# Seven block products for eight in both SwiGLU up projections, and a residual that lives in DRAM

## The chip, the cores and the metric

The kernel runs on one core of a Trainium2 chip. TensorE (PE) multiplies matrices into PSUM; VectorE (DVE), ScalarE (ACT) and GpSimd (POOL) compute element by element; SyncE (SP) issues DMAs. Each engine works through its own instructions in order, and semaphores tie the engines together. The metric is the time of one execution on the device in microseconds (us); the median of the runs is compared.

## The reference

A trunk of two layers on 1024 frames of 1024 channels: a mixer and a SwiGLU network each, both added to a residual `h`. The mixers (a convolution with pooling in layer 0, the HGRN2 recurrence in layer 1) compute what they did before. The hidden width D_FF is 2816. All is float32.

```
def rmsnorm(x, g):
    xf = x.astype(jnp.float32)
    y = xf * lax.rsqrt(jnp.mean(xf * xf, axis=-1, keepdims=True) + EPS)
    return (y * g.astype(jnp.float32)).astype(x.dtype)
...
def swiglu_ffn(h, w1, w3, w2):
    return (jax.nn.silu(h @ w1) * (h @ w3)) @ w2
...
    h = x
    for layer in range(DEPTH):
        hn = rmsnorm(h, norm_mix_g[layer])
...
        h = h + mix
        h = h + swiglu_ffn(rmsnorm(h, norm_ffn_g[layer]), ffn_w1[layer], ffn_w3[layer], ffn_w2[layer])
    return rmsnorm(h, final_g)
```

## The kernel before

Everything is kept with the channels on the 128 partitions and the frames along the free axis, in two halves `hf` of H = 512 frames. The residual is 16 SBUF tiles `hT[k][hf]` (8 channel groups k by 2 halves). Each large product has both operands split in a high and a low part (`split`, `load`: ACT casts the high part, DVE subtracts to get the low part) and is made in three passes, high by high, high by low, low by high (`gemm_steps`, L156 to L158). A product of one output tile over 8 channel groups is thus 24 matmuls of 128x512.

`Norm.gather` takes a finished residual tile, squares it on ACT (L218), adds the squares up on GpSimd (L220) and splits the tile times the norm's gain (L172, L173). The division by the RMS is applied later, to what the product gives: `rows` makes the broadcast tile `bcs`, by a chain of small DVE instructions, two products on TensorE and an ACT copy.

`ffn` walks over 22 hidden tiles j of 128 in blocks of 2, 4, 4, 4, 4, 4 (BLOCKS). For a hidden tile it loads the columns of w1 and w3 (512 KB each) and makes four products, p1 and p3 for both halves: 96 matmuls. DVE multiplies each by the RMS row (L586, L588), ACT applies the SiLU (L587), DVE multiplies the two (L589) and the result is split (L169, L170). At a block's end `down` multiplies the block's hidden tiles by w2: 16 output tiles, in a block of four of 12 matmuls each, and DVE adds each from PSUM to the residual (`add_residual`, L243). In the last block `norm_next.gather` follows each tile.

Products go on TensorE in the order of the program text (each behind the last one by `issue_after`); the other engines' instructions are put in order by a scheduler from the same text, and the tile pools set when buffers come free. Raw weights have two buffers (NRAW), their high and low parts three each (NSPLIT). Products take PSUM from four "g" banks (`gbank`), small things from four "m" banks. The page and its answers leave out the numbers in names, so `f0p` is any p1 or p3 of layer 0, `f0o` any down product there, and `wr`, `wh`, `wl` are a weight block raw, high and low.

## Time and profile before

| | before |
|---|---|
| median of 3 runs | 2366.84 us (2366.27 to 2366.86) |
| span of the profiled execution | 2363.6 us |
| PE busy | 2326.9 us, 98% |
| DVE busy | 1345.2 us, 57% |
| ACT busy | 600.5 us, 25% |
| POOL busy | 91.2 us, 4% |

The span is the time from the first to the last instruction of one profiled execution; the median of the timed runs is 3.2 us longer. Busy time is the time in which an engine executes an instruction. Slices of the span show PE at nine tenths or more from the second to the next-to-last fortieth. The rows below come from views of that execution: the page; the busy time by stretch (windows); the waits of an engine with what ended them; groups of instructions by line; and the timeline, where each row has a start, a duration, and in brackets the idle time before it and the instruction that ended it.

### The profile page before, as it was taken

What the parts mean: (1) busy time and instruction counts of PE and PEld (TensorE: products, weight loads), DVE (VectorE), ACT (ScalarE), POOL (GpSimd) and SP (SyncE); (2) the same over time, 40 slices, a digit from 0 to 9 for tenths busy, and PEclk for the clock granted to TensorE, in tenths of its full rate; (3) what the DMA queues carried; (4) which work ended last, traced back from release to release, by engine and by line L of the source; (5) the groups of instructions that cost most, each with busy time, mean ns of one, the idle gap of its engine ahead of it and who ended that gap; (6) DMA issues with size and microseconds to landing.
All of it is one profiled execution on the core that took longest, in us unless ns stands there. A gap on an engine that the chain in (4) does not pass through costs nothing.

```text
span 2363.6 us, 27955 instructions
## 1 busy us (share of the span) xinstructions
PE 2326.9 (98%) x11342; PEld 1959.9 (83%) x11342; DVE 1345.2 (57%) x2539; ACT 600.5 (25%) x962; POOL 91.2 (4%) x67
## 2 busy tenths in 40 slices
PE   8999999999999999999999999999999999999998
PEld 6887878888888888888898889887888888888888
DVE  7999953333333333567877778798433333333337
ACT  5223521112121211333232222215121211112126
POOL 1030200000000000110000000003000000000000
PEclk9999999999999999999999999999999999999999
DMA  4101211111111111121111111112111111111114
GB/s 155 55 24 50 72 54 45 54 45 46 44 53 54 45 54 45 63 72 46 36 46 36 54 45 45 37 36 63 40 50 54 45 54 45 54 41 51 53 45 143
DMA packets 181792, 126.89 MB, mean 54 GB/s; under 512 B 4692, under 2 KB 174880, under 8 KB 181664
## 3 DMA queue, kind: packets, MB, share of 16 engines
q1 hardware_dynamic: 181296, 124.94, 17.4%
q8 instruction: 89, 1.46, 0.2%
q14 instruction: 39, 0.32, 0.0%
q10 hardware_dynamic: 368, 0.17, 0.0%
HBM read 119.85 MB, written 4.19 MB: 52 GB/s over the span
## 4 chain that ended last, share of the span: by engine, by line
PE 89%; DVE 7%; issue 2%; ACT 1%; DMA 1%; SPq 0%; DVEq 0%; ACTq 0%
PE f1p L158 7%; PE f1p L156 7%; PE f1p L157 7%; PE f0p L156 7%; PE f0p L157 7%; PE f0p L158 7%; PE f1o L156 3%; PE f1o L158 3%; PE f1o L157 3%; PE f0o L157 3%; PE f0o L156 3%; PE f0o L158 3%; PE pl L750 3%; DVE y L375 2%; PE pq L156 1%
## 5 line engine op out<-in xcount | busy, mean ns | idle before, releaser
L138 ACT CAST wh<-wr 128x1024 fp32r<-128x1024 f32 x218 | 229.4, 1052 | 801.8 <-PE f1o L157 173.4
L139 DVE TENSOR_TENSOR wl<-wr,wh 128x1024 fp32r<-128x1024 f32 x216 | 267.9, 1240 | 33.9 <-ACT wh L138 33.3
L158 PE MATMUL f1p<-hn_nf_0h,wl 128*128 128x512 f32 x352 | 137.9, 392 | 3.3 <-DVE wl L139 3.3
L156 PE MATMUL f0p<-hn_nf_1h,wh 128*128 128x512 f32 x352 | 138.0, 392 | 0.0
L156 PE MATMUL f1p<-hn_nf_0h,wh 128*128 128x512 f32 x352 | 137.8, 392 | 0.1
L157 PE MATMUL f0p<-hn_nf_1l,wh 128*128 128x512 f32 x352 | 137.9, 392 | 0.0
L158 PE MATMUL f0p<-hn_nf_1h,wl 128*128 128x512 f32 x352 | 137.8, 392 | 0.0
L157 PE MATMUL f1p<-hn_nf_0l,wh 128*128 128x512 f32 x352 | 137.5, 390 | 0.0
L156 PE MATMUL f0p<-hn_nf_0h,wh 128*128 128x512 f32 x352 | 137.1, 389 | 0.0
L156 PE MATMUL f1p<-hn_nf_1h,wh 128*128 128x512 f32 x352 | 137.1, 389 | 0.0
L157 PE MATMUL f0p<-hn_nf_0l,wh 128*128 128x512 f32 x352 | 137.0, 389 | 0.0
L157 PE MATMUL f1p<-hn_nf_1l,wh 128*128 128x512 f32 x352 | 137.0, 389 | 0.0
L158 PE MATMUL f1p<-hn_nf_1h,wl 128*128 128x512 f32 x352 | 137.0, 389 | 0.0
L158 PE MATMUL f0p<-hn_nf_0h,wl 128*128 128x512 f32 x352 | 136.9, 389 | 0.0
L243 DVE TENSOR_TENSOR h<-h,f1o 128x512 f32<-128x512 f32 (+1 forms) x104 | 66.8, 645 | 115.3 <-PE f1o L158 114.9
L375 DVE SCALAR_TENSOR_TENSOR y<-a,dww,y 128x512 f32<-128x512 f32 (+1 forms) x150 | 130.8, 918 | 0.4
L243 DVE TENSOR_TENSOR h<-h,f0o 128x512 f32<-128x512 f32 x96 | 65.6, 684 | 110.6 <-PE f0o L158 110.5
L588 DVE TENSOR_TENSOR f1u<-f1p,bcs_nf 128x512 f32<-128x512 f32 x44 | 30.4, 691 | 170.0 <-PE f1p L158 170.0
L588 DVE TENSOR_TENSOR f0u<-f0p,bcs_nf 128x512 f32<-128x512 f32 x44 | 30.4, 691 | 170.0 <-PE f0p L158 170.0
L768 DVE COPY_PREDICATED S<-masks,pl 128x128 f32<-128x128 uint8 x288 | 94.1, 341 | 12.0 <-PE pl L750 10.4
L586 DVE TENSOR_TENSOR f1s<-f1p,bcs_nf 128x512 f32<-128x512 f32 x44 | 30.4, 692 | 106.0 <-PE f1p L158 104.5
L586 DVE TENSOR_TENSOR f0s<-f0p,bcs_nf 128x512 f32<-128x512 f32 x44 | 30.4, 691 | 105.7 <-PE f0p L158 104.1
(432 smaller groups left out, 5596.7 us busy)
## 6 DMA issues: line engine op xcount, KB each, us to landing
wr<-in_ffn_w SPq DMA_DIRECT2D x144, 512.0 KB, 3.7
wr<-in_hg_w_in SPq DMA_DIRECT2D x40, 512.0 KB, 4.0
wr<-in_cp_w_in SPq DMA_DIRECT2D x12, 512.0 KB, 3.9
wr<-in_cp_w_out SPq DMA_DIRECT2D x12, 512.0 KB, 3.4
wr<-in_hg_w_out SPq DMA_DIRECT2D x10, 512.0 KB, 3.7
x<-in_x SPq DMA_DIRECT2D x16, 256.0 KB, 5.6
out<-ob SPq DMA_DIRECT2D x8, 512.0 KB, 3.3
band<-in_c_band SPq DMA_DIRECT2D x1, 512.0 KB, 4.8
```

The source lines that it names most:

```text
L138: nc.scalar.copy(wh, raw)
L139: (leng or nc.vector).tensor_tensor(wl, raw, f32(wh), ALU.subtract)
L156: nc.tensor.matmul(ps, lh, xh, start=k == 0, stop=False)
L157: nc.tensor.matmul(ps, lh, xl, start=False, stop=False)
L158: mm = nc.tensor.matmul(ps, ll, xh, start=False, stop=k == len(xs) - 1)
L243: nc.vector.tensor_tensor(h, h, ps, ALU.add)
L375: nc.vector.scalar_tensor_tensor(acc, tap(at, j, t0, n), dww[:, j, c:c + 1], acc, ALU.mult, ALU.add)
L586: nc.vector.tensor_tensor(s, p1, rs[hf], ALU.mult)
L588: nc.vector.tensor_tensor(u, p3, rs[hf], ALU.mult)
L750: nc.tensor.matmul(pl[:, c], K[:, ch[cc]], M[:, :, cc * 64:(cc + 1) * 64], start=True, stop=True)
L768: nc.vector.copy_predicated(sv, mk.unsqueeze(1).to_broadcast([P, 2, 64 // w, w]), pl[:, :, j, :].rearrange("p c (b n) -> p c b n", n=w))
```

## The change

**Seven products.** With w1 and w3 side by side and both operands cut in two, the four outputs of a hidden tile, w1 and w3 by the two halves of frames, form a product of 2x2 blocks: even and odd channel groups are the inner blocks, the two weights the outer ones on one side, the halves of frames on the other. The class `Up` forms it in the Winograd form of Strassen's method: seven products of 12 matmuls, 84 for a hidden tile, on sums of blocks. The operand sums (`b11, b21, b22, t1..t4`) are made once for a layer in `PairNorm.gather`, per pair of residual tiles, when the second half's tiles are finished. The weight sums (s23: two blocks, one by GpSimd; s4; a2 in place) are made for each hidden tile by `sums`, and the output sums by `p1`, `p2` and `rest`: seven DVE additions from PSUM and an ACT copy in place of none. In the first block both hidden tiles' p1 and p2 go first, then the rest. Odd products take "g" banks, even ones "m" banks.

**The residual in DRAM.** The 16 SBUF tiles are gone; NACT, the ring of 512-frame tiles, grows from 48 to 72. The residual is `hd`, 8 DRAM tiles of 512 KB. A down product of all blocks but the last is copied from PSUM by ACT to a tile of the ring `su` (three of 128x1024, shared with the hidden tile's s and u), and GpSimd issues a DMA of 512 KB that adds it to `hd`. The mixer's first out-projection ("op", 16 tiles) and the HGRN2 out-projections (40 tiles) do the same in 256 KB through the ring `tmp` of three. Where a norm follows, the residual tile is fetched two ahead on SP's queue, added to by DVE, gathered and written back on ACT's queue. The HGRN2 out-projection of heads 4 to 7 for the second half of frames is made in one at the end.

```diff
-    NACT, NRAW, NSPLIT = 48, 2, 3
+    NACT, NRAW, NSPLIT = 72, 2, 3
...
+    def sooner(n=400):
+
+        return tc.high_priority(offset=n)
...
-    hT = [[hpool.tile([P, H], F32, tag=f"h{k}_{hf}", name=f"h{k}_{hf}") for hf in range(NH)] for k in range(KT)]
+    hd = [dram.tile([P, T], F32, name=f"hd{k}") for k in range(KT)]
...
+    class PairNorm(Norm):
...
+            if hf == 0:
+                z = ("b11", "b21")[k % 2]
+                ops[z][i] = split(h, f"{nm}{z}_{i}", scale=self.gain(k))
+            if hf == 0 or k % 2 == 0:
+                return
+            ge, go = self.gain(k - 1), self.gain(k)
+            (h11, h21), (h12, h22) = (x[k - 1:k + 1] for x in self.h)
+            t1 = temp(f"{nm}t1r_{i}")
+            nc.vector.tensor_tensor(t1, h12, h11, ALU.subtract)
+            nc.scalar.activation(t1, t1, AF.Copy, scale=ge)
+            ops["t1"][i] = split(t1, f"{nm}t1_{i}")
+            t2 = temp(f"{nm}t2r_{i}")
+            nc.vector.scalar_tensor_tensor(t2, h22, go, t1, ALU.mult, ALU.subtract)
+            ops["t2"][i] = split(t2, f"{nm}t2_{i}")
+            t4 = temp(f"{nm}t4r_{i}")
+            nc.vector.scalar_tensor_tensor(t4, h21, go, t2, ALU.mult, ALU.subtract)
+            ops["t4"][i] = split(t4, f"{nm}t4_{i}")
+            t3 = temp(f"{nm}t3r_{i}")
+            nc.scalar.activation(t3, h12, AF.Copy, scale=ge)
+            nc.vector.scalar_tensor_tensor(t3, h22, go, t3, ALU.mult, ALU.subtract)
+            ops["t3"][i] = split(t3, f"{nm}t3_{i}")
+            ops["b22"][i] = split(h22, f"{nm}b22_{i}", scale=go)
...
+    def accumulate(k, hf, ps, name):
+
+        o = temp(f"ev_{name}{k}_{hf}")
+        nc.scalar.copy(o, ps)
+        nc.gpsimd.dma_start(out=hd[k][:, half(hf)], in_=o, accum_op=ALU.add)
+
+    def fetch(k, hf, name):
+        h = staged(f"h_{name}{k}_{hf}")
+        nc.sync.dma_start(out=h, in_=hd[k][:, half(hf)])
+        return h
...
+    def add_residual(h, ps, t0=0, n=H):
+        nc.vector.tensor_tensor(h[:, t0:t0 + n], h[:, t0:t0 + n], ps, ALU.add)
+
+    def put_back(k, hf, h, eng=nc.scalar):
+        eng.dma_start(out=hd[k][:, half(hf)], in_=h)
...
-                            add_residual(2 * m2 + mo, hf, po)
-            # layer norm over the channels, then swish
+                            accumulate(2 * m2 + mo, hf, po, "op")
...
+        def wide(name):
+            return pool.tile([P, T], F32, tag="su", name=name, bufs=3)
+
+        class Up:
...
+            def sums(self):
+                self.fetch("w3", w3, self.tile("wraw", "w3", NRAW))
+                x = pool.tile([P, 1024], F32, tag="s23", name=f"{self.nm}s23", bufs=1)
+                xv = x.rearrange("p (two i b) -> p two i b", two=2, b=P)
+                a1, a2 = (self.raw[z].rearrange("p (i two b) -> p two i b", two=2, b=P) for z in ("w1", "w3"))
+                nc.gpsimd.tensor_tensor(xv[:, 1], a1[:, 0], a2[:, 0], ALU.subtract)
+                nc.vector.tensor_tensor(a2[:, 0], a2[:, 0], a2[:, 1], ALU.add)
+                nc.vector.tensor_tensor(xv[:, 0], a2[:, 0], a1[:, 0], ALU.subtract)
+                c = self.cast(self.run(x), "s23")
+                self.w[6], self.w[7] = (tuple(t[:, i:i + 4] for t in c) for i in (0, 4))
+                self.parts(self.cast(self.run(self.raw["w3"]), "a2"), 5, 4)
+                nc.vector.tensor_tensor(a1[:, 1], a1[:, 1], xv[:, 0], ALU.subtract)
+                self.w[3] = self.cast(a1[:, 1], "s4", 512)
+
+            def product(self, i):
+                xs = norm.ops[("b11", "b21", "b22", "t4", "t1", "t2", "t3")[i - 1]]
+                wh, wl = self.w[i]
+                ps = (gbank if i % 2 else mbank)(f"{self.nm}p{i}")
+                for k, (xh, xl) in enumerate(xs):
...
+            def p1(self):
+                self.r1 = (staged if self.first else temp)(f"{self.nm}p1")
+                nc.scalar.copy(self.r1, self.product(1))
...
+            def rest(self, scales=lambda: None):
...
+                nc.vector.tensor_tensor(u2, self.r1, self.product(6), ALU.add)
+                nc.vector.tensor_tensor(u3, u2, self.product(7), ALU.add)
+                nc.vector.tensor_tensor(self.u[:, l], u3, self.product(4), ALU.add)
+                if not self.first:
+                    self.gate(0, self.c11)
+                p5 = self.product(5)
+                nc.vector.tensor_tensor(u2, u2, p5, ALU.add)
+                nc.vector.tensor_tensor(self.u[:, r], u3, p5, ALU.add)
+                nc.vector.tensor_tensor(self.s[:, r], u2, self.product(3), ALU.add)
+                scales()
...
-            for j in range(j0, j0 + nb):
-                u1, u3 = load(*cols(w1, j)), load(*cols(w3, j))
-                for hf in range(NH):
-                    p1, p3 = gbank(f"{nm}p1_{j}_{hf}"), gbank(f"{nm}p3_{j}_{hf}")
-                    gemm(p1, u1, 0, xs[hf])
...
+            for j in range(j0, j0 + nb) if b else ():
+                x = Up(j)
+                x.sums()
+                x.p1()
+                x.p2()
+                x.rest()
...
             if not last:
-                spans = [[(0, 0, H), (1, 0, H)]]
...
+                    w = load(*cols(w2, mg, per, j0, nb))
+                    os = [wide(f"{nm}ev{b}_{mg + i}") for i in range(per)]
+                    for hf in range(NH):
+                        for i in range(per):
+                            nc.scalar.copy(os[i][:, half(hf)], product(mg, i, hf, w))
+                    for i in range(per):
+                        nc.gpsimd.dma_start(out=hd[mg + i], in_=os[i], accum_op=ALU.add)
...
-        OUT_AT = {3: ([0, 1],), 7: ([2, 3], [4, 5])}
+        OUT_AT = {3: (([0, 1], (0, 1)),), 7: (([2, 3], (0, 1)), ([4, 5], (0,)))}
...
-        for hf in range(NH):
-            for _ in project_out([6, 7], [hf], True):
+        ahead = Ahead("ho", [(k, hf) for hf in range(NH) for k in range(KT)])
+        for hds, hf in (([6, 7], 0), ([4, 5, 6, 7], 1)):
+            for _ in project_out(hds, [hf], ahead):
                 pass
```

What stands on three engines where the prediction looks; names are as above, with `f_9` for the tenth hidden tile (its `w` are raw weights, `p` a PSUM product, `s` and `u` the two outputs, `a1`, `s23`, `a2`, `s4` weight sums, h and l their parts).

DVE in the middle of a block of four of layer 0, before: all of it between the products of one hidden tile and the next.

```order
L586 TENSOR_TENSOR f0s_0_3428<-f0p_5_0_3378,bcs_nf_2594 128x512
L588 TENSOR_TENSOR f0u_0_3429<-f0p_5_0_3379,bcs_nf_2594 128x512
L589 TENSOR_TENSOR f0s_0_3428<-f0s_0_3428,f0u_0_3429 128x512
L170 TENSOR_TENSOR f0g_0l<-f0s_0_3428,f0g_0h 128x512
L586 TENSOR_TENSOR f0s_1_3488<-f0p_5_1_3438,bcs_nf_2686 128x512
L139 TENSOR_TENSOR wl_3562<-wr_3560,wh_3561 128x1024
L588 TENSOR_TENSOR f0u_1_3489<-f0p_5_1_3439,bcs_nf_2686 128x512
L589 TENSOR_TENSOR f0s_1_3488<-f0s_1_3488,f0u_1_3489 128x512
L139 TENSOR_TENSOR wl_3624<-wr_3622,wh_3623 128x1024
L170 TENSOR_TENSOR f0g_1l<-f0s_1_3488,f0g_1h 128x512
```

And now, from the first sum of one hidden tile's outputs to a weight split of the next one:

```order
L749 TENSOR_TENSOR f_8u_4441<-f_8p_4410,f_8p_4443 128x512
L704 TENSOR_TENSOR f_9w_4536<-f_9w_4536 128x4x128
L750 TENSOR_TENSOR f_8u_4442<-f_8u_4441,f_8p_4457 128x512
L691 TENSOR_TENSOR f_9a1l<-f_9w_4530,f_9a1h 128x1024
L705 TENSOR_TENSOR f_9s_4538<-f_9w_4536,f_9w_4530 128x512
L751 TENSOR_TENSOR f_8u<-f_8u_4442,f_8p_4471 128x512
L709 TENSOR_TENSOR f_9w_4530<-f_9w_4530,f_9s_4538 128x4x128
L739 TENSOR_TENSOR f_8u<-f_8u,bcs_nf_2935 128x512
L740 TENSOR_TENSOR f_8s<-f_8s,f_8u 128x512
L755 TENSOR_TENSOR f_8u_4441<-f_8u_4441,f_8p_4493 128x512
L756 TENSOR_TENSOR f_8u<-f_8u_4442,f_8p_4493 128x512
L691 TENSOR_TENSOR f_9s23l<-f_9s_4538,f_9s23h 128x1024
```

Two weight splits and eight operations for a hidden tile have become 22 instructions, and the sum of the next tile's raw weights (L704, in place) now stands right behind the first output sum (L749), ahead of the sums that finish the present tile.

The down products of the block of two of layer 0, on DVE, before:

```order
L243 TENSOR_TENSOR h_0_91<-h_0_91,f0o_0_0_0_0_2836 128x512
L139 TENSOR_TENSOR wl_2972<-wr_2970,wh_2971 128x1024
L170 TENSOR_TENSOR f0g_1l<-f0s_1_2820,f0g_1h 128x512
L243 TENSOR_TENSOR h_0_93<-h_0_93,f0o_0_1_0_0_2844 128x512
L243 TENSOR_TENSOR h_0_95<-h_0_95,f0o_0_2_0_0_2852 128x512
L243 TENSOR_TENSOR h_0_97<-h_0_97,f0o_0_3_0_0_2860 128x512
L243 TENSOR_TENSOR h_1_92<-h_1_92,f0o_0_0_1_0_2868 128x512
L243 TENSOR_TENSOR h_1_94<-h_1_94,f0o_0_1_1_0_2876 128x512
L243 TENSOR_TENSOR h_1_96<-h_1_96,f0o_0_2_1_0_2884 128x512
L243 TENSOR_TENSOR h_1_98<-h_1_98,f0o_0_3_1_0_2892 128x512
```

And now, on ACT:

```order
L173 CAST f0g_1h<-f_1s 128x512
L819 COPY f0ev_1_3102<-f0o_0_1_0_0_3113 128x512
L819 COPY f0ev_2_3103<-f0o_0_2_0_0_3121 128x512
L819 COPY f0ev_0_3101<-f0o_0_0_1_0_3137 128x512
L819 COPY f0ev_1_3102<-f0o_0_1_1_0_3145 128x512
L819 COPY f0ev_2_3103<-f0o_0_2_1_0_3153 128x512
L690 CAST f_2s23h<-f_2s_3259 128x1024
L819 COPY f0ev_3_3104<-f0o_0_3_0_0_3129 128x512
L819 COPY f0ev_3_3104<-f0o_0_3_1_0_3161 128x512
L819 COPY f0ev_4_3179<-f0o_4_0_0_0_3183 128x512
L819 COPY f0ev_5_3180<-f0o_4_1_0_0_3191 128x512
```

The additions to the residual have left DVE; ACT copies to the tiles `f0ev`, and the copies of the fourth product (`f0ev_3`) stand behind the second half's first three, where the ring's first tile has to come free. GpSimd, which had nothing between the norms of the two mixers, now has, at a block of four and the next one's start:

```order
L821 DMA hd_90<-f0ev_0_3837 128x1024
L821 DMA hd_91<-f0ev_1_3838 128x1024
L703 TENSOR_TENSOR f_6s_4103<-f_6w_4095,f_6w_4101 128x512
L821 DMA hd_92<-f0ev_2_3903 128x1024
L821 DMA hd_93<-f0ev_3_3904 128x1024
L821 DMA hd_94<-f0ev_4_3969 128x1024
L821 DMA hd_95<-f0ev_5_3970 128x1024
L821 DMA hd_96<-f0ev_6_4035 128x1024
L821 DMA hd_97<-f0ev_7_4036 128x1024
L703 TENSOR_TENSOR f_7s_4248<-f_7w_4240,f_7w_4246 128x512
```

The accumulating DMAs (L821) stand in one queue with the sums of the weights (L703): that of the next block's second hidden tile stands behind all eight.

DVE at the end of layer 0's mixer, where its last residual tiles become the operands of the feed-forward network, before:

```order
L243 TENSOR_TENSOR h_1_100<-h_1_100,oa_0_1_2398 128x512
L173 SCALAR_TENSOR_TENSOR hn_nf_1l<-h_1_98,prm,hn_nf_1h 128x512
L173 SCALAR_TENSOR_TENSOR hn_nf_1l<-h_1_100,prm,hn_nf_1h 128x512
L243 TENSOR_TENSOR h_1_102<-h_1_102,oa_1_1_2419 128x512
L139 TENSOR_TENSOR wl_2510<-wr_2508,wh_2509 128x1024
L173 SCALAR_TENSOR_TENSOR hn_nf_1l<-h_1_102,prm,hn_nf_1h 128x512
L243 TENSOR_TENSOR h_1_104<-h_1_104,oa_0_1_2446 128x512
L173 SCALAR_TENSOR_TENSOR hn_nf_1l<-h_1_104,prm,hn_nf_1h 128x512
L243 TENSOR_TENSOR h_1_106<-h_1_106,oa_1_1_2467 128x512
L139 TENSOR_TENSOR wl_2700<-wr_2698,wh_2699 128x1024
L173 SCALAR_TENSOR_TENSOR hn_nf_1l<-h_1_106,prm,hn_nf_1h 128x512
```

And now, for the last pair of channel groups:

```order
L317 TENSOR_TENSOR h_oa_1_2580<-h_oa_1_2580,oa_0_1_2656 128x512
L691 TENSOR_TENSOR f_0s4l<-f_0w_2739,f_0s4h 128x512
L177 SCALAR_TENSOR_TENSOR hn_nf0b_2l<-h_oa_1_2524,prm,hn_nf0b_2h 128x512
L317 TENSOR_TENSOR h_oa_1_2600<-h_oa_1_2600,oa_1_1_2674 128x512
L274 TENSOR_TENSOR hn_nf0t1r_2691<-h_oa_1_2580,h_oa_0_2321 128x512
L704 TENSOR_TENSOR f_1w_2985<-f_1w_2985 128x4x128
L705 TENSOR_TENSOR f_1s_2987<-f_1w_2985,f_1w_2745 128x512
L278 SCALAR_TENSOR_TENSOR hn_nf0t2r_2698<-h_oa_1_2600,prm,hn_nf0t1r_2691 128x512
L174 TENSOR_TENSOR hn_nf0t_3l<-hn_nf0t1r_2691,hn_nf0t_3h 128x512
L281 SCALAR_TENSOR_TENSOR hn_nf0t4r_2704<-h_oa_0_2345,prm,hn_nf0t2r_2698 128x512
L174 TENSOR_TENSOR hn_nf0t_3l<-hn_nf0t2r_2698,hn_nf0t_3h 128x512
L285 SCALAR_TENSOR_TENSOR hn_nf0t3r_2710<-h_oa_1_2600,prm,hn_nf0t3r_2710 128x512
```

Two additions and two splits a pair have become eleven instructions, with the weight sums of the first two hidden tiles among them.

## Rows read from the trace of the kernel before

**Rows 1.** The page: the span, busy times by engine, and the chain by engine.

```profile
span 2363.6 us, 27955 instructions
...
PE 2326.9 (98%) x11342; PEld 1959.9 (83%) x11342; DVE 1345.2 (57%) x2539; ACT 600.5 (25%) x962; POOL 91.2 (4%) x67
...
PE 89%; DVE 7%; issue 2%; ACT 1%; DMA 1%; SPq 0%; DVEq 0%; ACTq 0%
```

**Rows 2.** Windows, us: five engines' busy time (instructions), granted clock, DMA share, GB/s.

```profile
210.00:279.00 69.00, 68.94 (x307) 55.78 (x306) 64.42 (x113) 32.14 (x48) 9.09 (x6) 1.00 0.17 54
279.00:325.00 46.00, 42.89 (x184) 34.93 (x183) 35.10 (x59) 17.87 (x27) 12.45 (x9) 0.93 0.23 69
410.00:943.00 533.00, 533.00 (x2353) 441.36 (x2352) 191.90 (x245) 92.17 (x115) 0.00 (x0) 1.00 0.16 50
1550.00:1600.00 50.00, 50.00 (x270) 41.95 (x269) 45.32 (x125) 9.43 (x18) 0.00 (x0) 1.00 0.11 32
1600.00:1650.00 50.00, 46.55 (x202) 36.92 (x201) 42.72 (x71) 27.89 (x43) 21.80 (x14) 0.97 0.22 64
```

**Rows 3.** Windows, the same columns: the first 5.6 us after a wait of TensorE.

```profile
309.40:315.00 5.60, 5.51 (x13) 4.14 (x14) 3.24 (x6) 1.83 (x3) 0.00 (x0) 0.50 0.00 0
```

**Rows 4.** Waits of PE: what it waited for, us in total, times, longest.

```profile
PE bc_nf L196 <- DVE dg_nf L194: 3.1, 1, 3.1
```

**Rows 5.** The page, costliest groups: busy us, mean ns | idle before.

```profile
L138 ACT CAST wh<-wr 128x1024 fp32r<-128x1024 f32 x218 | 229.4, 1052 | 801.8 <-PE f1o L157 173.4
L139 DVE TENSOR_TENSOR wl<-wr,wh 128x1024 fp32r<-128x1024 f32 x216 | 267.9, 1240 | 33.9 <-ACT wh L138 33.3
...
L243 DVE TENSOR_TENSOR h<-h,f0o 128x512 f32<-128x512 f32 x96 | 65.6, 684 | 110.6 <-PE f0o L158 110.5
```

**Rows 6.** Groups by line in 410 to 943 us, the same columns.

```profile
L589 DVE TENSOR_TENSOR f0s<-f0s,f0u 128x512 f32<-128x512 f32 x33 | 22.8, 692 | 3.8 <-DVE f0u L588 0.5
...
L587 ACT ACTIVATE f0s<-f0s 128x512 f32<-128x512 f32 x33 | 20.8, 632 | 74.4 <-DVE f0s L586 74.4
```

**Rows 7.** Timeline of DVE, 308 to 330 us: start, duration, instruction [idle, releaser].

```profile
311.61 0.69 DVE L586 TENSOR_TENSOR f0s<-f0p,bcs_nf 128x512 f32<-128x512 f32 x1 [1.57 <-ACT bcs_nf L238]
312.21 0.68 DVE L588 TENSOR_TENSOR f0u<-f0p,bcs_nf 128x512 f32<-128x512 f32 x1
313.00 0.69 DVE L589 TENSOR_TENSOR f0s<-f0s,f0u 128x512 f32<-128x512 f32 x1
314.37 0.69 DVE L170 TENSOR_TENSOR f0g_0l<-f0s,f0g_0h 128x512 fp32r<-128x512 f32 x1 [0.68 <-ACT f0g_0h L169]
...
325.96 1.23 DVE L139 TENSOR_TENSOR wl<-wr,wh 128x1024 fp32r<-128x1024 f32 x1 [1.71 <-ACT wh L138]
327.10 0.68 DVE L586 TENSOR_TENSOR f0s<-f0p,bcs_nf 128x512 f32<-128x512 f32 x1
```

**Rows 8.** Timeline of DVE, 268 to 290 us, while GpSimd adds at L220.

```profile
279.99 2.32 DVE L139 TENSOR_TENSOR wl<-wr,wh 128x1024 fp32r<-128x1024 f32 x1
282.23 0.74 DVE L173 SCALAR_TENSOR_TENSOR hn_nf_0l<-h,prm,hn_nf_0h 128x512 fp32r<-128x512 f32 x1
```

**Rows 9.** Timeline of POOL (GpSimd) in the same stretch.

```profile
277.89 3.33 POOL L220 TENSOR_TENSOR nacc_nf<-nacc_nf,sq_nf 128x512 f32<-128x512 f32 x2
284.37 1.49 POOL L220 TENSOR_TENSOR nacc_nf<-nacc_nf,sq_nf 128x512 f32<-128x512 f32 x1 [3.15 <-ACT sq_nf L218]
```

**Rows 10.** The page, DMA: queue q1, and issues with us from issue to landing.

```profile
q1 hardware_dynamic: 181296, 124.94, 17.4%
...
wr<-in_ffn_w SPq DMA_DIRECT2D x144, 512.0 KB, 3.7
...
out<-ob SPq DMA_DIRECT2D x8, 512.0 KB, 3.3
```

**Rows 11.** Timeline of DVE, 1709 to 1712 us: a split that frees a weight buffer.

```profile
1710.24 1.22 DVE L139 TENSOR_TENSOR wl<-wr,wh 128x1024 fp32r<-128x1024 f32 x1 [0.21 <-ACT wh L138]
```

**Rows 12.** Timeline of SP, 1710 to 1716 us: the load that takes that buffer.

```profile
1711.49 0.37 SPq L137 DMA_DIRECT2D wr<-in_ffn_w  x1
```

More of the change, by code (lines that the diff above doesn't have):

```diff
@@ new lines, in half, with __init__, __call__ @@
+    def half(hf):
+        return slice(hf * H, (hf + 1) * H)
+    def accumulate(k, hf, ps, name):
[6 more added lines that the diff above has]
+        return h
+    class Ahead:
+        def __init__(self, name, order):
+            self.name, self.order, self.got = name, list(order), {}
+        def __call__(self, k, hf):
+            i = self.order.index((k, hf))
+            for kk in self.order[:i + 3]:
+                if kk not in self.got:
+                    self.got[kk] = fetch(*kk, self.name)
+            return self.got[k, hf]
@@ L349, in layer0_mixer @@
                 glu(at, 0, wv, wg, [1])
+            for kk, h in held.items():
+                put_back(*kk, h, nc.sync)
             for i in range(0, 9, 5):
@@ L359, in layer0_mixer @@
             nc.sync.dma_start(out=bprev, in_=a["c_bprev"].rearrange("p (g t) -> p g t", t=16))
-            yc = [pool.tile([P, T], F32, tag=f"y{c}", name=f"y{c}", bufs=1) for c in range(NC4)]
-            ybuf = [[y[:, hf * H:(hf + 1) * H] for hf in range(NH)] for y in yc]
+            ybuf = [[staged(f"y{c}_{hf}") for hf in range(NH)] for c in range(NC4)]
+            for y in sum(ybuf[:NC4 - 1], []):
+                nc.gpsimd.memset(y[:, :1], 0.0)
             def tap(at, j, t0, n):
@@ L591, in ffn, with product @@
+            xs = [[hid[j][hf] for j in range(j0, j0 + nb)] for hf in range(NH)]
             last = b == len(BLOCKS) - 1
             per = 8 // nb
+            spans = [[(0, 0, H)], [(1, 0, H)]] if done is None else LAST_SPANS
+            ahead = Ahead(nm, [(k, hf) for hf in range(NH) for k in range(KT)])
+            def product(mg, mo, hf, w, t0=0, n=H):
+                po = gbank(f"{nm}o{b}_{mg}_{mo}_{hf}_{t0}")[:, :n]
+                gemm(po, w, mo, [tuple(x[:, t0:t0 + n] for x in xhl) for xhl in xs[hf]])
+                return po
@@ L610, in ffn @@
-            for span in spans:
                 for mg in range(0, KT, per):
                     w = load(*cols(w2, mg, per, j0, nb))
-                    for sp in span:
-                        down(mg, sp[0], w, *sp[1:])
-                if last and done is not None:
-                    for _ in pending:
-                        pass
-                    pending = done(*span[0])
+                    os = [wide(f"{nm}ev{b}_{mg + i}") for i in range(per)]
+                    for hf in range(NH):
+                        for i in range(per):
+                            nc.scalar.copy(os[i][:, half(hf)], product(mg, i, hf, w))
@@ new lines, in ffn @@
+                    for i in range(per):
+                        nc.gpsimd.dma_start(out=hd[mg + i], in_=os[i], accum_op=ALU.add)
+            else:
+                for span in spans:
+                    for mg in range(0, KT, per):
+                        with sooner():
+                            w = load(*cols(w2, mg, per, j0, nb))
+                        for sp in span:
+                            down(mg, sp[0], w, *sp[1:])
+                    if done is not None:
+                        for _ in pending:
+                            pass
+                        pending = done(*span[0])
@@ L833, in hgrn, with project_out @@
         ogs = [[None] * HEADS for _ in range(NH)]
-        def project_out(hds, halves, final=False):
+        def project_out(hds, halves, ahead=None):
             n = len(hds)
@@ L853, in filler @@
                 yield from project(hd + 1, tiles)
-            for hds in OUT_AT.get(hd, ()):
-                yield from project_out(hds, range(NH))
+            for hds, halves in OUT_AT.get(hd, ()):
+                yield from project_out(hds, halves)
         pr = new_tiles()
```

222 lines of the change are left out of this document (148 added, 74 removed).

## The prediction

> **What bounds the kernel now.** I read the page first: PE is busy for 2326.9 of 2363.6 us, and 89% of the chain that ended last is PE [rows 1]. That is an average, so next come the stretches. Between 410 and 943 us, blocks of four hidden tiles and their down products, PE is busy for all of 533.00 us with 2353 matmuls, 0.2265 us each, while DVE works for 191.90 us, ACT for 92.17 and GpSimd not at all [rows 2]. There the time is the count of matmuls. At the two entries of the feed-forward networks it isn't: PE is short of 3.1 us in 279 to 325 and of 3.45 us in 1600 to 1650 [rows 2], the first nearly all the chain of small DVE instructions behind the RMS row [rows 4]. DVE is at 64.42 of 69 us just ahead of the first entry and at 45.32 of 50 ahead of the second [rows 2], so what the change gives DVE to do there comes on top of an engine that is nearly full. After the wait in the first entry the granted clock is at 0.50 (1.2 of 2.4 GHz) for 5.6 us [rows 3], which costs about 2.8 us more.
>
> **Term 1: the matmuls.** A hidden tile takes 84 for 96, 44 hidden tiles in two layers: 528 fewer. At 0.2265 us [rows 2] that is 119.6 us, if nothing else ends later. The order shows them gone, so that the change doesn't do what it says is excluded. 2363.6 - 119.6 = 2244.0 us of span; the median of the runs stands 3.2 us over the span, so the floor is 2247.
>
> **Term 2: the blocks of four, nothing.** DVE's work for a hidden tile rises from 8 operations of 512 (0.69 us) and 2 splits of 1024 (1.24 us) [rows 5, 6], 8.0 us, to 19 and 3, 16.8 us, against 84 x 0.2265 = 19.0 us of PE. The down products free DVE of 16 additions. So DVE has room; what counts is a loop. The in-place weight sum (L704) waits for GpSimd's (L703), this one for the loads of the next tile's w1 and w3, and the later load for the buffer that the present tile's s4 split frees. From L704 to the end of that split are 20 DVE instructions, in order. Those of 512 start 0.60 us apart, the splits take 1.14 to the next start, and one that needs the result before it starts after 0.79 [rows 7]: 17 x 0.60 + 3 x 1.14 + some 1.1 for such pairs = 14.7 us. The load is issued 0.03 us behind the split that frees its buffer [rows 11, 12] and lands after 3.7 us [rows 10]. GpSimd's sum of 512 isn't in the trace; an addition of 512 takes it 1.5 to 1.7 us beside a working DVE [rows 9], and DVE stands still for this one, so I take 1.4, with 0.2 for the two handovers. The loop is 14.7 + 3.7 + 1.6 = 20.0 us, 1 us over PE's 19.0. In a block three such passes lie between four tiles, 3 us, and in the 43.5 us of down products before them (192 x 0.2265) DVE has only four weight splits, so that the first tile's weights stand ready some 3 to 4 us early. PE just doesn't wait. ACT has three casts of 1.05 and six operations of 0.63 us a tile, 7 us, and 16 more copies in the down products [rows 5, 6]: it is hidden twice over. Each microsecond more in the loop costs up to 3 us a block.
>
> **Term 3: the accumulating DMAs.** Nothing in the trace adds in DRAM. From below: 512 KB written to DRAM land after 3.3 us, 512 KB read after 3.7 [rows 10]. In throughput, 124.94 MB took 17.4% of 16 engines over 2363.6 us [rows 1, 10], 411 us, so 512 KB take 1.7 us of all engines; the addition reads two streams and writes one, which makes 3.4 to 5.2 us of engines and, by the read and the write in sequence, 3.3 + 3.7 = 7 us to landing. From above I have no row: several times that. Two are issued every 10.9 us in a block of four, so one served behind another needs up to 5.4 us each for no backlog; I take the lower half. The ring of three leaves room there: the copy of product 6 needs the tile of products 1 and 3, whose DMA was issued 7.5 us earlier, and four PSUM banks hold PE free for 8 us more. Nothing for the eight large blocks. In the two small ones four tiles are needed of three: product 4's copy waits for the DMA of products 1 and 5, and PE meets it at product 8. Products are 6 x 0.2265 = 1.36 us; the copy of product 5 ends at 7.5 us, the DMA lands 7 us later, a copy more makes 15.2, and PE is there at 9.5. That is some 5.7 us, twice (tiles 4 to 7 again), of which I count one, since DVE is late there anyway and catches up: **+5 us a layer, +10**, between +2 and +20.
>
> **Term 4: the entry of the first network.** For a pair of channel groups DVE has eleven operations for four: 11 x 0.69 = 7.6 us. While GpSimd adds squares DVE is held: the same split takes 0.74 us clear of it, and a weight split 2.32 for 1.22 beside it [rows 8, 9]; two such additions a pair make some 9 us, four pairs 36, and the weight sums and splits of the first two hidden tiles 10 more: 46 us. PE has beside that 8 products of 12 for the second half and four products on the first half's operands, 12 x 12 x 0.2265 = 32.6 us, and then needs the last pair's t1, which comes some 42 us in. PE waits 8 to 12 us there, then for the later sums at DVE's pace, then as before for the RMS row (3.1 us for one half [rows 4], now both halves, between the seventh product and the gates): 4 to 5, and 1 to 3 before the first down product. With one or two drops of the clock at 2.8 us [rows 3] that is 16 to 26 us, say 20, for 6 before: **+14**.
>
> **Term 5: the entry of the second.** The same work, but DVE brings a lag from the end of the recurrence (45.32 of 50 us busy [rows 2]) and the residual now comes by fetch. I add some 9 us to the 20 and take off the 5 of before (3.45 idle, and 1.5 by the clock of 0.97 over 50 us): **+24**, between +10 and +40.
>
> **Term 6: the rest.** The last block's tiles, the mixer's and HGRN2's are fetched and written back, 16 issues on ACT each time at 0.37 us, if an issue there costs what it does on SP [rows 12], beside an ACT at 32.14 of 69 us [rows 2]; a fetch behind an accumulation to the same tile can be late; more tiles free DVE of additions. **+6**, between -2 and +15.
>
> **The sum.** 2363.6 - 119.6 + 10 + 14 + 24 + 6 = 2298 us of span, and with 3.2 around it **2301 us**. About half of what is given back is at two places where DVE, not PE, sets the pace.
>
> **The rivals.** *A, slower: the accumulating DMAs hold the tiles.* Served one after another at L each, the eight of a block take 8 L, against 43.5 us of down products, 7.5 us of ring and 8 us of PSUM, 59 us; what is beyond that PE waits for, in eight blocks. At L = 9 it is 13 x 8 = 104 us: 2405 us. The 65 us that are left of the gain are gone at L = 8.4 us. Against it speak the 1.7 us that 512 KB take of the engines now; for it, that no row shows this kind of DMA, that it is issued by an engine which DVE is seen to share something with [rows 8, 9], and that GpSimd's weight sum stands in the same queue. The Trainium skill has a rule that speaks for it ("SBUF — State Buffer", "SBUF: two separate sides"): while DVE runs certain copies of fp32 in SBUF, GpSimd can't write the descriptors of DMAs that it issues, and these wait. By that rule each would start late by a DVE instruction, 0.7 to 1.3 us here, which the ring's 7.5 us hold; the sum would stay. The skill also says that an addition in a DMA costs its two reads ("Collectives: The Full Stack", "The bandwidth ceiling: the fold count and why AG ≠ RS ≠ AR"); by that, estimated, twice 1.7 us, no rival.
>
> *B: the loop of term 2 is longer.* If w1 and w3 land one behind the other (two loads, 6.2 us for 3.7) it is 22.5 us, 3.5 over PE's, 10.5 a block less the lead of 3.5: 7 us in ten blocks of four, 70 us: 2371. At half of that, 2336. For it: one long queue on SP, which now also has fetches. Against it: loads land after 3.7 us now though they are issued in twos [rows 10].
>
> *C: the entries cost twice the 38 us* (each a second lag, a further drop of the clock): 2339.
>
> *D: the whole gain.* DVE runs ahead at the entries as the products of the first half cover it, and the small blocks hide in it: 10 us for all, 2257.
>
> **How the numbers follow.** The forecast (2280 to 2325) 0.52; D (2250 to 2280) 0.14; C and the weak form of B (2325 to 2362) 0.16; the strong form of B near 2367 0.04; A or B beyond it 0.14. Within 0.2% (4.7 us, about what a measurement of this kernel tells from no change) is the 0.04; faster 0.82; slower 0.14. The range holds 8 in 10 from 2254 to 2364: it leaves A and no change out, and the lowest 0.02.
>
> **What would show it.** In the profile after: 528 fewer matmuls; in a block of four no wait of PE, a tile's L704 20 us behind the last one's, POOL's sums at 1.4 us; accumulating DMAs landing within 7 us; PE's waits gathered around the two entries (for t1, the RMS row, `f0ev`), 20 and 29 us with their clock. It is wrong if PE waits for weight splits in the blocks (B), for ACT copies behind `ev` (A), or if an entry's share is under 10 or over 50 us.

## The result

The changed kernel takes 2338.52 us (median of 4 runs, 2337.94 to 2340.82) beside 2366.56 before on the same chip: a ratio of 0.9886, 95% interval 0.9872 to 0.9900. It is faster by 28 us, where 66 were forecast. The direction holds and the time lies in the wide range (2254 to 2364), but above the forecast's bracket of 2280 to 2325: more than half of the expected gain is missing. The profiled execution has a span of 2336.4 us, against 2298 in the sum.

The page of the kernel after, the lines that answer to [rows 1]:

```profile
span 2336.4 us, 28603 instructions
...
PE 2238.8 (96%) x10814; PEld 1877.1 (80%) x10814; DVE 1569.8 (67%) x2932; ACT 838.6 (36%) x1354; POOL 268.6 (11%) x253
...
PEclk9999989999999999999999999998899999999999
...
q0 software_dynamic: 19584, 56.63, 15.3%
```

528 matmuls are gone (11342 to 10814). PE is busy for 88 us less but idle for 61 us more, and its clock falls in two places, at a seventh and at seven tenths of the span. Queue q0 is GpSimd's, with the accumulating DMAs. To see where the time went I cut both spans at the same events, each the start of a matmul in the timeline, and took the lengths between them. "Due" is the length before less the matmuls that left the stretch, at 0.2265 us each. The change makes 48 matmuls of heads 4 and 5 later, but those of their other half move up in their place: 156 matmuls of `ho` start behind the recurrence's last product `pl` before and 159 after, so only three, 0.7 us, leave its stretch.

| stretch | before | due | after | over |
|---|---|---|---|---|
| start to the second out-projection `oa` | 249.1 | 249.1 | 257.5 | 8.4 |
| `oa` to layer 0's first up product | 45.3 | 45.3 | 58.6 | 13.3 |
| to its first down product (block of two) | 52.8 | 47.4 | 57.6 | 10.2 |
| those down products | 21.7 | 21.7 | 28.3 | 6.6 |
| five blocks of four | 652.6 | 598.2 | 599.5 | 1.3 |
| HGRN2 to its first out-projection `ho` | 303.1 | 303.1 | 300.8 | -2.3 |
| to the recurrence's last product `pl` | 254.4 | 253.7 | 270.9 | 17.2 |
| to layer 1's first up product | 40.1 | 40.8 | 60.1 | 19.3 |
| to its first down product | 52.0 | 46.6 | 54.9 | 8.3 |
| those down products | 21.7 | 21.7 | 29.1 | 7.4 |
| to the end | 670.8 | 616.4 | 619.1 | 2.7 |
| sum | 2363.6 | 2244.0 | 2336.4 | 92.4 |

The blocks of four give the whole gain. The recurrence's stretch, from the first `ho` to the last `pl`, shows the loss plainly, before and after: the same work of PE to three matmuls, but PE idle for 10.4 us and busy for 6.2 us more, at a granted clock of 0.98.

```profile
1324.60:1579.00 254.40, 254.23 (x1479) 222.80 (x1477) 205.86 (x588) 65.32 (x133) 0.00 (x0) 1.00 0.14 40
```

```profile
1302.30:1573.20 270.90, 260.46 (x1476) 225.92 (x1474) 188.77 (x555) 87.09 (x171) 31.22 (x36) 0.98 0.37 73
```

Windows of the kernel after, in the columns of [rows 2]: layer 0's blocks of four, one of the two stretches of out-projections under the recurrence, the wait for the operand sums, and a block of two's down products.

```profile
402.00:980.00 578.00, 576.93 (x2545) 477.32 (x2544) 334.66 (x466) 195.34 (x276) 58.70 (x56) 1.00 0.41 94
...
1302.30:1340.00 37.70, 32.95 (x163) 27.02 (x162) 8.94 (x16) 14.22 (x24) 13.87 (x16) 0.95 0.87 143
...
316.10:345.00 28.90, 21.75 (x75) 16.70 (x76) 26.36 (x35) 16.23 (x26) 7.32 (x5) 0.76 0.25 73
...
373.70:402.00 28.30, 24.63 (x98) 18.88 (x97) 8.76 (x11) 11.17 (x20) 7.33 (x8) 0.94 0.56 106
```

In the first row PE misses 1.07 of 578 us. In the second DVE works for only 8.94 of 37.70 us and ACT for 14.22, yet PE is short of 4.75: no engine is full, so somebody probably waits for something that isn't an engine. The waits of ACT in the kernel after (waited for, us in total, times, longest) name it:

```profile
ACT ev_ho L295 <- DMA hd<-ev_ho: 31.9, 24, 3.8
...
ACT f1ev L819 <- DMA hd<-f1ev: 12.2, 6, 2.5
```

`ev_ho` are the tiles in which HGRN2's out-projections go to the accumulating DMA, a ring of three that the recurrence's own temporaries share. The timeline of ACT at the start of that second window (start, duration, instruction, idle time and what ended it):

```profile
1303.94 0.59 ACT L295 COPY ev_ho<-ho 128x512 f32<-128x512 f32 x1
1305.30 0.59 ACT L295 COPY ev_ho<-ho 128x512 f32<-128x512 f32 x1 [0.77 <-PE ho L162]
1306.61 0.59 ACT L295 COPY ev_ho<-ho 128x512 f32<-128x512 f32 x1 [0.72 <-PE ho L162]
1310.47 0.59 ACT L295 COPY ev_ho<-ho 128x512 f32<-128x512 f32 x1 [3.27 <-DMA hd<-ev_ho]
```

Three copies follow PE at its 1.36 us a product; the fourth waits for the first one's DMA, which frees its tile 6.5 us after the copy began.

### The profile page after: what moved, and what is told of

Read it like the earlier page. It is cut to its first block, busy times and chain, and to the rows that moved or that the text cites. A ratio compares the mean times of both kernels' runs of the same rounds, so it can differ in the third digit from the quotient of the medians.

```text
span 2336.4 us, 28603 instructions
## 1 busy us (share of the span) xinstructions
PE 2238.8 (96%) x10814; PEld 1877.1 (80%) x10814; DVE 1569.8 (67%) x2932; ACT 838.6 (36%) x1354; POOL 268.6 (11%) x253
## 3 DMA queue, kind: packets, MB, share of 16 engines
q0 software_dynamic: 19584, 56.63, 15.3%
HBM read 137.67 MB, written 77.59 MB: 92 GB/s over the span
## 4 chain that ended last, share of the span: by engine, by line
PE 53%; issue 25%; DVE 10%; DMA 4%; POOL 2%; ACT 1%; SPq 0%; POOLq 0%; DVEq 0%; ACTq 0%
PE f1o L162 3%; PE f1o L160 3%; PE f1o L161 3%; PE f0o L161 3%; PE f0o L162 3%; PE f0o L160 3%; DVE y L458 3%; POOL hd L296 1%; DVE wl L143 1%; PE op L160 1%; PE op L161 1%; PE op L162 1%; DMA f_3w<-in_ffn_w 1%; PE f_5p L720 1%; PE f_21p L720 1%
## 5 line engine op out<-in xcount | busy, mean ns | idle before, releaser
L143 DVE TENSOR_TENSOR wl<-wr,wh 128x1024 fp32r<-128x1024 f32 x130 | 160.0, 1231 | 99.1 <-ACT wh L142 98.5
L142 ACT CAST wh<-wr 128x1024 fp32r<-128x1024 f32 x132 | 138.7, 1051 | 142.0 <-PE pg L161 19.6
L458 DVE SCALAR_TENSOR_TENSOR y<-a,dww,y 128x512 f32<-128x512 f32 x180 | 137.6, 817 | 0.4
L160 PE MATMUL f1o<-f1g_1h,wh 128*128 128x512 f32 (+1 forms) x208 | 74.9, 360 | 2.7 <-ACT f1ev L819 2.0
L162 PE MATMUL f1o<-f1g_1h,wl 128*128 128x512 f32 (+1 forms) x208 | 74.2, 357 | 0.0
L161 PE MATMUL f1o<-f1g_1l,wh 128*128 128x512 f32 (+1 forms) x208 | 74.1, 356 | 0.0
L966 PE MATMUL pl<-M,K 128*128 128x192 f32 x384 | 71.4, 329 | 2.1 <-DVE M L953 2.0
L160 PE MATMUL f0o<-f0g_1h,wh 128*128 128x512 f32 x176 | 69.4, 394 | 3.0 <-ACT f0ev L819 3.0
L160 PE MATMUL f1o<-f1g_0h,wh 128*128 128x512 f32 x176 | 69.3, 394 | 1.2 <-ACT f1g_0h L173 0.8
L161 PE MATMUL f1o<-f1g_0l,wh 128*128 128x512 f32 x176 | 69.3, 394 | 0.8 <-DVE f1g_0l L174 0.8
L821 POOL DMA_DIRECT2D hd<-f1ev x40 | 34.7, 875 | 238.8 <-ACT f1ev L819 238.5
```

Of the source, the lines that this page charges most:

```text
L142: nc.scalar.copy(wh, raw)
L143: (leng or nc.vector).tensor_tensor(wl, raw, f32(wh), ALU.subtract)
L160: nc.tensor.matmul(ps, lh, xh, start=k == 0, stop=False)
L161: nc.tensor.matmul(ps, lh, xl, start=False, stop=False)
L162: mm = nc.tensor.matmul(ps, ll, xh, start=False, stop=k == len(xs) - 1)
L458: nc.vector.scalar_tensor_tensor(acc, tap(at, j, t0, n), dww[:, j, c:c + 1], acc, ALU.mult, ALU.add)
```

## The experiments

All are edits of the changed kernel; each was timed beside the kernel before on its chip (2366.06 to 2366.63 us). The expectations stand as they were written.

**The ring of three in HGRN2.**

```diff
-        o = temp(f"ev_{name}{k}_{hf}")
+        o = (staged if name.startswith("ho") else temp)(f"ev_{name}{k}_{hf}")
```

> One edit to the changed kernel: the 40 accumulated tiles of the HGRN2 out-projections are copied to the ring of 72 tiles for the ring of three. Theory A: in the changed kernel a tile of the ring of three is held for 0.6 us of copy, some 0.9 us of issue and 5.4 us to landing, 6.9 us, so three products pass in 6.9 us where TensorE needs 3 x 1.36 = 4.1; ScalarE waits (31.9 us in all), then TensorE, and its clock falls. The stretch from the last down product of layer 0 to layer 1's first up product, 631.6 us, comes down to about 605, and the time from 2338.5 to 2308 to 2318 us. Rival B (the stretch is long because the out-projection of heads 4 and 5 for the second half of frames was moved behind the recurrence, which lacks it as cover): ScalarE's waits go, the stretch keeps all but 5 us, time 2333 to 2339.

2314.24 us (2308.82 to 2315.51), ratio 0.9777 (0.9762 to 0.9792): 24 us faster than the changed kernel. ACT's copies in the same place, and the window that answers to the second one above:

```profile
1306.96 0.59 ACT L295 COPY ev_ho<-ho 128x512 f32<-128x512 f32 x1 [0.77 <-PE ho L162]
1308.32 0.59 ACT L295 COPY ev_ho<-ho 128x512 f32<-128x512 f32 x1 [0.77 <-PE ho L162]
```

```profile
1301.30:1339.00 37.70, 37.70 (x223) 33.93 (x222) 16.18 (x40) 17.34 (x33) 13.91 (x16) 1.00 0.87 167
...
1301.30:1554.80 253.50, 253.35 (x1475) 222.29 (x1474) 188.23 (x555) 87.02 (x171) 31.33 (x37) 1.00 0.38 78
```

The fourth copy and all after it follow PE, which makes 223 matmuls in the 37.70 us for 163, at the full clock. Lengths: from the first `ho` to the last `pl` 253.5 us for 270.9, which is its due (253.7), with PE busy in all but 0.15 us of it (second row); and to the first up product 54.9 for 60.1. Theory A holds, and the DMA share of 0.87 is the same in both: it is the number of tiles, not the DMA engines' throughput.

**The addition in the DMA.**

```diff
-        nc.gpsimd.dma_start(out=hd[k][:, half(hf)], in_=o, accum_op=ALU.add)
+        nc.gpsimd.dma_start(out=hd[k][:, half(hf)], in_=o)
```

(and the same in the blocks of the feed-forward networks)

> The DMAs that add to the residual in DRAM only write there: the addition of these products to the residual is left out, and nothing else; the order of all engines is the same. Theory A': it is the addition in the DMA that makes it 5.4 us to landing; as a plain write it lands after about 3.3 us, a ring tile is held 4.8 us, and the stretch of HGRN2 loses some 12 to 18 us, the blocks of two some 3 us each: time 2315 to 2325. Rival: a DMA issued by GpSimd takes the 5.4 us whatever it does with the bytes: 2336 to 2340, no difference.

2306.30 us (2305.02 to 2307.47), 32 us faster, more than expected. The DMA issues and GpSimd's issuing instruction, of the kernel after and then of this one:

```profile
L296 POOL DMA_DIRECT2D hd<-ev_ho x40 | 34.7, 896 | 539.2 <-ACT ev_ho L295 537.7
...
hd<-f0ev POOLq DMA_DIRECT2D x40, 512.0 KB, 5.4
...
hd<-ev_ho POOLq DMA_DIRECT2D x40, 256.0 KB, 5.4
```

```profile
L296 POOL DMA_DIRECT2D hd<-ev_ho x40 | 21.6, 541 | 532.2 <-ACT ev_ho L295 528.3
...
hd<-f0ev POOLq DMA_DIRECT2D x40, 512.0 KB, 2.9
...
hd<-ev_ho POOLq DMA_DIRECT2D x40, 256.0 KB, 2.8
```

Without the addition a DMA lands after 2.8 to 2.9 us for 5.4, counted from the start of its issue, and the issue takes GpSimd 541 ns for 896. The rings of three are then nearly long enough: 254.7 us from `ho` to `pl`, 22.5 and 23.9 in the blocks of two. So the price of the addition and the length of the rings are two sides of one wait.

**The moved out-projection.** The changed kernel makes heads 4 to 7 of the second half in one, behind the recurrence. Undone:

```diff
-        OUT_AT = {3: (([0, 1], (0, 1)),), 7: (([2, 3], (0, 1)), ([4, 5], (0,)))}
+        OUT_AT = {3: (([0, 1], (0, 1)),), 7: (([2, 3], (0, 1)), ([4, 5], (0, 1)))}
...
-        for hds, hf in (([6, 7], 0), ([4, 5, 6, 7], 1)):
+        for hds, hf in (([6, 7], 0), ([6, 7], 1)):
```

> One edit to the changed kernel: the out-projection of heads 4 and 5 for the second half of frames goes back under the recurrence, as in the kernel before, and the last one has heads 6 and 7 alone for both halves. Rival B expects 10 to 15 us less (2324 to 2329). Theory A expects that eight more accumulations go through the ring of three while the recurrence runs, 0.9 us each over TensorE's need: no gain, 2336 to 2350.

2351.90 us (2348.70 to 2356.77), 13 us slower. Rival B of e1_ring's expectation falls. Whether the ring is the reason was asked with the wide one:

> The edits of e1_ring and e3_out together: the wide ring, and the out-projection of heads 4 and 5 for the second half of frames back under the recurrence. If e3_out was slower only because it sent eight more tiles through the ring of three, the products now give cover and the stretch from the first HGRN2 out-projection to layer 1's first up product, 308.4 us in e1_ring and 294.5 before, comes down by 5 to 11 us: 2303 to 2309. Rival: the recurrence has cover enough, and its end is set by VectorE and ScalarE: within 4 us of e1_ring's 2314.

2329.14 us (2322.15 to 2329.97), 15 us slower than with the wide ring alone. Both sides of that expectation missed. The recurrence has cover enough (253.3 us from `ho` to `pl` for 253.5), but the stretch behind it grows from 54.9 to 68.2. Waits of PE in this kernel:

```profile
PE ho L160 <- DVE h_ho L317: 11.2, 4, 4.6
PE f_0p L718 <- DVE h_ho L317: 11.0, 1, 11.0
```

The move doesn't carry work out of the recurrence: 159 matmuls of `ho` stand behind its last product in both kernels. It puts 48 of them beside DVE's operand sums, which take some 9 us for a pair of tiles (`t1` to the next `t1` 9.8 and 8.9 us here). Two products of 12 matmuls take PE 5.4 us, two of 6 take 2.7: the longer ones are cover for DVE, and without them PE waits.

**The operand sums.** With the wide ring, t1 to t4 left out:

```diff
-            t1 = temp(f"{nm}t1r_{i}")
...
-            ops["t3"][i] = split(t3, f"{nm}t3_{i}")
+            for z, y in (("t1", "b11"), ("t2", "b21"), ("t4", "b11"), ("t3", "b21")):
+                ops[z][i] = ops[y][i]
```

> e1_ring, and the operand sums t1 to t4 are left out: the four products that use them take the plain operands b11 and b21 in their place, so that VectorE has three operations less a tile pair for each sum. All products, weight sums and DMAs are there. Theory: at both entries VectorE sets the pace with the operand sums. The stretch from the first product of the mixer's second out-projection to the first down product, 116.3 us, falls to 98 to 102; in layer 1 the tail behind the recurrence and the entry, 109.9 us, to 96 to 100: time 2314 to about 2286. Rival: the entries wait for the residual's fetches and for the chain of the RMS row, and keep 10 us more than that: 2298 to 2306.

2279.53 us (2277.63 to 2279.93), 35 us faster than with the sums. From `oa` to the first down product 99.9 us for 116.3 with the wide ring (98 to 102 expected), in layer 1 from the last `pl` on 93.6 for 109.9. So the sums, for each pair of tiles eight operations of DVE and six of ACT, cost 33 us at the two entries together. DVE sets the pace: in the changed kernel it works for 26.36 of 28.90 us there and ACT for 16.23 (third window of the result). The part from `oa` to the first up product stays at 54.9 us for 45.3 due: that is another wait.

**The fetches ahead of the entry.**

```diff
-        nc.sync.dma_start(out=h, in_=hd[k][:, half(hf)])
+        (nc.gpsimd if name == "oa" and hf == 0 else nc.sync).dma_start(out=h, in_=hd[k][:, half(hf)])
```

> One edit to the changed kernel: the residual tiles that the first half of the mixer's second out-projection adds to are fetched on GpSimd's queue for SyncE's; all other orders are the same. Theory: in the changed kernel these fetches stand behind five weight loads which wait for buffers, the first is issued at 272.1 us, 13 us after the accumulation that it needs was issued, and TensorE waits 7.6 us for it and loses 2.8 more by its clock: time 7 to 11 us less, 2328 to 2332. Rival: DVE, which is busy for most of that stretch, ends it anyway and takes the gain back at the entry of the feed-forward network: 2335 to 2339.

2334.06 us (2333.23 to 2334.49), 4 us less, though the intervals of the two ratios (0.9850 to 0.9880 and 0.9872 to 0.9900) overlap. The stretch in question is 58.2 us for 58.6, and what was gained lies in other stretches, up to 2.3 us each, which the edit doesn't touch. Waits of PE between 250 and 320 us, of the kernel after and of this one:

```profile
PE oa L160 <- DVE h_oa L317: 7.6, 1, 7.6
...
PE f_0p L718 <- ACT hn_nf0t_1h L173: 3.8, 1, 3.8
```

```profile
PE f_0p L718 <- ACT hn_nf0t_1h L173: 6.8, 1, 6.8
PE oa L160 <- DVE h_oa L317: 4.0, 1, 4.0
```

The first wait is 3.6 us shorter and the next, for an operand sum, 3.0 longer: a stall moved. The same edit without the operand sums:

> e6_nosums (the operand sums t1 to t4 left out) and the early fetches of e4_fetch. With the sums, the earlier fetch shortened TensorE's first wait from 7.6 to 4.0 us and the wait in front of the first up product grew from 3.8 to 6.8: VectorE took the gain back. Theory: without the sums nobody takes it back, and the stretch from the first product of the second out-projection to the first up product falls from 54.9 to 50 to 52 us, time 2279.5 to 2274 to 2277. Rival: the accumulation that the fetch waits for ends it, or VectorE's order does: 54 to 56 us and no change.

The stretch falls to 51.8 us, as expected; the time, 2279.25 us (2274.70 to 2280.41), isn't the 2274 to 2277 expected and can't be told from 2279.53 in runs that lie this far apart. What remains of the first wait (4.6 us) is DVE's order, in which the addition to the first tile stands behind the last of the layer norm.

**The blocks of two.** With the wide ring in HGRN2, the fourth of a group's tiles last:

```diff
-                    for hf in range(NH):
-                        for i in range(per):
-                            nc.scalar.copy(os[i][:, half(hf)], product(mg, i, hf, w))
+                    for part in (range(3), range(3, per)) if per > 3 else (range(per),):
+                        for hf in range(NH):
+                            for i in part:
+                                nc.scalar.copy(os[i][:, half(hf)], product(mg, i, hf, w))
```

> e1_ring, and in the blocks of two the fourth of a group's output tiles is made last, behind both halves of the first three, so that the first tile of the ring has begun its DMA three products before it is needed again. Theory (the step on the small blocks): ScalarE's copy of the fourth tile waits for the DMA of the first, and TensorE behind it; that goes, and the two stretches from the first down product to the second block, 25.1 and 28.8 us in e1_ring for 21.7 of TensorE's work, come to 22 to 25: time 2306 to 2311. Rival: the stretch is long because the next tile's weights come late: no change.

2313.02 us (2312.14 to 2314.95), no difference; 27.9 and 27.1 us for 25.1 and 28.8. The theory that one DMA's early start is enough falls. The timeline of ACT and of PE in that kernel's first block of two:

```profile
395.71 0.59 ACT L820 COPY f0ev<-f0o 128x512 f32<-128x512 f32 x1 [1.91 <-DMA hd<-f0ev]
399.81 2.05 ACT L820 COPY f0ev<-f0o 128x512 f32<-128x512 f32 x4 [3.51 <-DMA hd<-f0ev]
```

```profile
400.45 0.50 PE L160 MATMUL f0o<-f0g_0h,wh 128*128 128x512 f32 x1 [2.44 <-ACT f0ev L820]
```

The wait has moved into the second group of four. So this order doesn't help either; others weren't tried. Taking the wait away instead, by 256 KB at a time through the ring of 72 tiles (the edit of `accumulate` now takes in these tiles too):

```diff
+                    if per > 2:
+                        for hf in range(NH):
+                            for i in range(per):
+                                accumulate(mg + i, hf, product(mg, i, hf, w), f"{nm}b{b}_")
+                        continue
```

> e1_ring, and in the blocks of two the 16 down products go out like those of HGRN2, as 256 KB each through the ring of 72 tiles, so that no copy waits for a DMA there. Theory: what the two stretches from the first down product to the second block have over TensorE's 21.7 us (3 to 7 us each in the runs so far, with a fall of the clock in it) is the ring of three: they come to 22 to 24 us, time 2304 to 2310 for 2314. Rival: the DMAs' throughput itself, seen as a full share of the DMA engines there, delays the next tile's weights: within 3 us of 2314.

2303.70 us (2302.07 to 2304.43), ratio 0.9734 (0.9720 to 0.9749). The down products take 22.5 and 25.6 us; in layer 1 what is left over is 1.6 us of PE's waits for the split of the hidden tile and a clock of 0.93. This version beats both kernels: 62 us faster than before, 35 faster than the change.

> e8_small and e4_fetch together, a candidate that computes all. Since e4_fetch left its stretch as it was, 2302 to 2310, no better than e8_small by more than 3 us.

2304.61 us (2303.67 to 2305.45): no better; the stretch of the fetch is 58.6 us for 58.8.

**One part alone.** The residual in DRAM with the eight products, norm and loop of the kernel before:

> The residual in DRAM alone: the changed kernel with the eight products of the kernel before, its norm and its loop over the hidden tiles, and all that the change does to the residual (accumulating DMAs, fetches, rings of three, the moved out-projection). Theory: the residual's move costs what the changed kernel lost outside the operand sums: 8 us to the second out-projection, 4 to 10 in it, 3 to 7 at each block of two, 16 in the recurrence and 10 to 15 behind it, and nothing in the blocks of four: 40 to 55 us over before, 2407 to 2422; the seven products then bring 70 to 85 us. Rival: with eight products and no operand sums to form, TensorE has slack and hides it: under 20 us over before, up to 2386.

2414.08 us (2410.46 to 2415.11), ratio 1.0203 (1.0186 to 1.0220): 48 us slower than before. The DRAM residual alone is a loss, and the seven products bring 76 us on top of it. ACT waits 36.1 us for `ev_ho` here:

```profile
ACT ev_ho L295 <- DMA hd<-ev_ho: 36.1, 25, 4.4
...
ACT f0ev L810 <- DMA hd<-f0ev: 11.2, 5, 3.9
```

The recurrence takes 269.2 us from `ho` to `pl`, as in the changed kernel, so its loss has nothing to do with the products.

## Why the prediction was half right

**Terms 1 and 2 hold.** The matmuls left, and the blocks of four keep everything. The loop through the weight sums was put at 20.0 us. The timeline of DVE in a block of four after, at the in-place sums:

```profile
536.18 0.69 DVE L704 TENSOR_TENSOR f_7w<-f_7w 128x512 f32<-128x512 f32 x1 [4.09 <-POOL f_7s L703]
...
556.27 0.69 DVE L704 TENSOR_TENSOR f_8w<-f_8w 128x512 f32<-128x512 f32 x1 [4.28 <-POOL f_8s L703]
...
576.33 0.69 DVE L704 TENSOR_TENSOR f_9w<-f_9w 128x512 f32<-128x512 f32 x1 [4.25 <-POOL f_9s L703]
```

20.09 and 20.06 us from one to the next. That is over PE's 19.0, DVE stands 4 us in it for GpSimd, and PE waits 1.1 us in five blocks, since the lead of three to four microseconds lasts for the three passes. Rival B is out.

**Term 3 was right in its mechanism, and a little short.** The DMAs land after 5.4 us where 7 was taken, and the ring of the blocks of four holds (`f0ev` and `f1ev` in large blocks: no wait of PE). The blocks of two lose 6.6 and 7.4 us where 5 was counted, of which e8_small gives back 5.7 and 3.6: the DVE lag that was to take the second wait back isn't there (DVE works for 8.76 of 28.30 us), and PE's clock falls in it (0.94 over the window).

**The step that failed is term 6**, "+6" for the rest. The rest lost 27.3 us: 8.4 ahead of `oa`, 17.2 under the recurrence, 1.7 in what remains. I had worked out in term 3 when a ring of three holds PE, for the tiles of the down products, and didn't ask the same of the other ring of three, `tmp`, through which HGRN2's 40 tiles go: in the sum their wait stands at nothing. The long ring takes 17.4 us out of the recurrence's stretch and 5.2 out of the one behind it, and 24 from the time (e1_ring). The numbers were all there. With the 7 us to landing of term 3 and a copy of 0.6, three products pass in 7.6 us, against 3 x 1.36 = 4.1 of PE's: 3.5 us for each three, some 47 us for 40 products, if PE has nothing else to do in between. Measured, a tile is held 6.3 us (median of the 40: 0.6 of copy, 0.3 to the issue, 5.4 from the issue's start to the landing; the 6.9 in the expectation of e1_ring counts the issue's 0.9 twice), which makes 2.2 us for each three and some 30. Less was lost; that steps of the recurrence lie between the later products would explain it, but no run shows that by itself. Rival A named this mechanism (the accumulating DMAs hold the tiles), with a price by the DMAs' throughput and at the large blocks: the wrong place, and the wrong limit. With both rings long the time is 2303.7, 3 us from the forecast; that the other terms' misses nearly cancel is part of that: against the table's due, term 4 then stands at 23 for 14, term 5 at 22 for 24, term 3 at 5 for 10, and term 6 at its 6.

**Term 4 was short, term 5 nearly right.** From `oa` to the first down product the loss is 23.5 us for +14, in layer 1 from the last `pl` on 27.6 for +24, 5.2 of them by HGRN2's ring (e1_ring). Forecast 38, measured 51, of which the operand sums are 33 (e6_nosums against e1_ring). Term 4 has no wait ahead of the out-projection's additions, where PE stands 7.6 us; term 6 says only that a fetch can be late. The fetch stands on SP behind five weight loads that wait for buffers, and DVE waits 3.7 us for it; the rest is DVE's order, which e4_fetch and e11_nosums_fetch leave at 4.0 and 4.6 us. Term 5 came near in part by luck: the products that the change puts beside DVE's sums give cover, a part of the change that I had read and not priced, and without it the time is 13 to 15 us longer (e3_out, e5_ring_out). Chance is also that the time meets rival C's 2339: C has the two entries at twice 38 us, and they cost 51.

**What stays open.** The 8.4 us ahead of `oa`. About half shows in the first 131 us, where the first products' operands now stand behind the chain of the RMS row in DVE's order and 16 tiles are written to DRAM; the rest lies between there and `oa`. None of it was taken apart by a run. Of the 9.5 us that term 4 lacks, e11_nosums_fetch takes back 3.1, without the operand sums; with them no run took any.

The Trainium skill's rule on descriptors ("SBUF — State Buffer", "SBUF: two separate sides") is one of certain fp32 copies on DVE, and DVE's work beside these DMAs is nearly all sums and splits (TENSOR_TENSOR and SCALAR_TENSOR_TENSOR): no run here tests it. With the long rings of e8_small the DMAs land after 5.2 to 5.7 us, those of the blocks of two, where 16 of 256 KB follow one another, after 6.9 and 7.5, and no engine is seen to wait for them.

## What to carry to other kernels

When a result goes out through a DMA that adds, a tile of its ring is busy from the copy's start to the landing: count the copy and the time from the start of the issue to the landing, divide by the ring's length, and compare with the time of one product at every place where the ring is used, the shortest product first. A stretch in which no engine is full and the tensor engine still waits may be held by a ring, and a longer ring, without a faster DMA, may be all that it needs. And when several edits come together, price also those that look like housekeeping (an order, a moved product, a queue): here one of them was worth 13 to 15 us.
